# Mixer A's lowest score level by multiplied rows and a product with ones; small products traced one at a time between large ones; an even spread of steps

## The chip, the cores and the metric

The kernel runs on one core of a Trainium2 chip. A core has TensorE (matrix products), VectorE, ScalarE and GpSimd (element-wise work), and SyncE, which issues DMAs. The metric is the device time of one execution in microseconds (us); the median of several runs is compared. In the profile PE is TensorE's products, PEld its weight loads, DVE is VectorE, ACT ScalarE, POOL GpSimd, and SP SyncE. A line such as L588 is line 588 of the kernel before.

## What is computed

The reference is a trunk of two layers over 512 tokens of width 2048, in float32. Layer A is a gated linear recurrence (HGRN2), layer B attention with a forget gate. Each layer is: RMS norm, one input projection, the mixer with 16 heads of 128, a norm per head, times SiLU of a gate, an output projection, plus the residual.

```python
# layer A, per head; blocks of HG_BLOCK = 16 tokens, state S carried from block to block
b = jnp.cumsum(gc, axis=-2)                                  # gc: log of the forget gate
diff = b[..., :, None, :] - b[..., None, :, :]
decay = jnp.exp(jnp.where(mask, diff, -jnp.inf))             # mask: s <= t
A = jnp.einsum('bhtd,bhsd,bhtsd->bhts', qc, kc, decay)
o = A @ vc + (qc * jnp.exp(b)) @ S
# layer B, per head
s = q @ k.T * d**-0.5 + F[t] - F[s]                          # s <= t
o = softmax(s) @ v
```

So a score of layer A is the sum over the 128 channels d of q[t,d] k[s,d] exp(b[t,d] - b[s,d]).

## The kernel before

**Large groups.** Everything lies transposed: channels on the 128 partitions, the 512 tokens along the free dimension. A projection is cut into groups of 512 output columns (`group`, L220 to L249). A group runs over 16 steps of the contraction, here called k-steps (`kt`). Weights and activations are each split into a rounded high half and the low rest (`split`, L439: a cast on ScalarE, a subtraction on VectorE), and a product is three: high-high, high-low, low-high. A k-step has 4 output banks `gm0` to `gm3` times 3 products = 12 products of 512 columns. After the last k-step each bank is evacuated by VectorE or ScalarE (`evac`).

**The output products** (`out_product`, L833) have one such group, in which finished heads are split and prepared (`y_split`, `quick_prep`), and six pairs of groups by Strassen's scheme (`quick`, L269), with 256-column products whose weights are seven sums of quarters. VectorE makes these sums (`w_sums`, L153, tile `wm`) and they are split into `w7h` and `w7l`.

**Order.** For A the groups are `q0 v0 q1 q2 v1 q3 g0 q4 v2 q5 q6 v3 q7 g1 g2 g3`, for B `v0 q0 q1 q2 v1 g0 q3 q4 v2 g1 q5 q6 v3 q7 g2 g3`; a q group brings q and the key or gate side of two heads, a v group the values of four, a g group the gates of four. An output product ends each phase.

**Mixers as steps.** A head's mixer is a Python generator (`mix_a`, L606; `mix_b`, L922), and each `yield` ends a step. After each k-step `group` adds `rate` to `due` and calls `pump`, which runs that many steps of the first two open heads in turn, the second from when the first has reached "half". RATE_A is 2 and RATE_B 1. What a step traces stands in the program there. The order of tracing is a priority: a scheduler then places each engine's instructions by it and by when it reckons that their inputs are ready, so the products of a step can come later than they are traced, and some stand alone between large ones. `need` runs steps early where an evacuation wants a buffer, `flush` (L103) runs what is left at the end of a phase.

**Scores of A.** Tokens of a window of 128 are compared at levels: 1 (neighbours in groups of 4), 4, 16, 64, and then across windows. For d = 0 to 3 tokens back, level 1 forms q times the decay (tile `pr`, L628; tile `e` holds the decays of one, two and three tokens), splits q, `pr` and k, and multiplies them on TensorE: per window 3 products of 320 columns (L588 to L590), a full 128 by 320 table, of which `put_scores` (L575) copies the entries d tokens back into `at` with predicated copies under masks. Then q and k are multiplied by their decays in place (L640, L645) for the next level. Levels 4 and 16 have 3 products of 192 columns for each window, level 64 three of 128 columns for each of two windows; the scores across windows go to `ah` and `al`. `attend` (L425) multiplies by the values with 12 products, and `out_norm` (L396) sums squares with a product by `ones` (`sum_parts`, L328) and writes `Y[h]` (L407).

**Banks.** Four PSUM banks (`mx`, L71) serve all of the mixers' products; the four `gm` banks serve the large groups.

## Time and profile before

| | |
|---|---|
| median of 3 runs | 2014.63 us (2012.73 to 2015.29) |
| the profiled execution | 2013.94 us, its span 2012.2 us |
| instructions | 28874 |
| chain that ended last, by engine | PE 84%, DVE 7%, DMA 4%, issue 2%, ACT 1%, POOL 1% |
| large products (L238 to L244) in that chain | 17% + 17% + 17% + 6% + 6% + 6% |
| predicated copies (L583) | 448, 108.8 us of VectorE |
| granted TensorE clock | 0.994 of full speed |

The span is the time from the first to the last instruction of the program; the execution's time also has what lies around it. A busy share is the part of the span in which an engine had an instruction under way. A row of the timeline gives start, length, engine, line, operation, result and operands, and shapes; a bracket at its end gives the idle time before it and what ended it. A row of waits gives who waited for whom, the sum, the number of times and the longest. TensorE's products overlap, so the length of one is more than the time that it takes from its neighbours; the distance between two starts shows that.

### The profile page before, as it was taken

Reading aid. Unit: us, or ns where it says so; the run is one execution under the profiler, and the core shown is the slowest. Engines: PE = TensorE matmul, PEld = TensorE weight load, DVE = VectorE, ACT = ScalarE, POOL = GpSimd, SP = SyncE. Lnnn points to the kernel's source line nnn. Section 1 sums busy time; section 2 is a strip of 40 time slices with the busy share of each in tenths; the row PEclk is TensorE's granted clock in tenths of the full one; section 3 lists DMA queues with packets and bytes.
Section 4 is the critical chain, followed back from the end, with each engine's and each line's share of the span. In section 5 each row is a group of like instructions: output and inputs, shape, how many; then the busy total and the mean of one; then the engine's idle time right before and its main releaser. Section 6 shows DMA issues by size and latency. Waiting matters only on the chain.

```text
span 2012.2 us, 28874 instructions
## 1 busy us (share of the span) xinstructions
PE 1978.6 (98%) x10218; PEld 1696.5 (84%) x10218; DVE 1558.8 (77%) x3321; ACT 1130.1 (56%) x2311; POOL 172.8 (9%) x301
## 2 busy tenths in 40 slices
PE   9999999999999999989999999999999999999898
PEld 7888888888888888869987888888888888888898
DVE  7968987979798889698873677776766676688877
ACT  5646655657566466654443555655555556576332
POOL 3303110202122030000000000000000000000000
PEclk9999999999999999999999999999999999999999
DMA  5222222222222222244433222333233232223443
GB/s 189 74 87 82 74 84 75 83 79 79 84 74 74 74 84 84 84 142 140 149 118 95 94 87 87 95 89 95 84 89 93 92 95 89 90 84 111 132 156 105
DMA packets 61696, 195.01 MB, mean 97 GB/s; under 512 B 7904, under 2 KB 8032, under 8 KB 61552
## 3 DMA queue, kind: packets, MB, share of 16 engines
q1 hardware_dynamic: 61408, 193.17, 30.8%
q8 instruction: 80, 1.31, 0.3%
q14 instruction: 64, 0.52, 0.1%
q10 hardware_dynamic: 144, 0.01, 0.0%
HBM read 184.73 MB, written 8.42 MB: 96 GB/s over the span
## 4 chain that ended last, share of the span: by engine, by line
PE 84%; DVE 7%; DMA 4%; issue 2%; ACT 1%; POOL 1%; SPq 0%; DVEq 0%; ACTq 0%; POOLq 0%
PE gm L244 17%; PE gm L242 17%; PE gm L243 17%; PE gm L238 6%; PE gm L240 6%; PE gm L239 6%; DMA wr<-in_wb_q 2%; DVE w7l L441 2%; PE mx L590 2%; PE mx L589 2%; PE mx L588 1%; DMA wr<-in_wa_q 1%; PE mx L435 1%; PE mx L436 1%; PE mx L434 1%
## 5 line engine op out<-in xcount | busy, mean ns | idle before, releaser
L242 PE MATMUL gm<-xh,wh 128*128 128x512 f32 x1664 | 650.6, 392 | 0.1
L243 PE MATMUL gm<-xl,wh 128*128 128x512 f32 x1664 | 649.8, 391 | 0.0
L244 PE MATMUL gm<-xh,wl 128*128 128x512 f32 x1664 | 610.3, 392 | 1.1 <-DVE wl L441 1.1
L242 PEld LDWEIGHTS gm<-xh,wh 128*128 128x128 f32 x1664 | 313.1, 188 | 63.1 <-ACT wh L440 0.3
L243 PEld LDWEIGHTS gm<-xl,wh 128*128 128x128 f32 x1664 | 313.2, 188 | 62.7
L244 PEld LDWEIGHTS gm<-xh,wl 128*128 128x128 f32 x1664 | 311.3, 188 | 63.6 <-DVE wl L441 2.3
L440 ACT CAST wh<-wr 128x512 fp32r<-128x512 f32 x288 | 177.3, 620 | 155.7 <-PE gm L243 113.8
L441 DVE TENSOR_TENSOR wl<-wr,wh 128x512 fp32r<-128x512 f32 x288 | 204.7, 714 | 66.8 <-ACT wh L440 56.8
L147 ACT ACTIVATE wh<-wr,v_b_norm_w 128x256 fp32r<-128x256 f32 (+1 forms) x192 | 111.7, 584 | 186.4 <-PE gm L243 152.3
L148 DVE SCALAR_TENSOR_TENSOR wl<-wr,v_b_norm_w,wh 128x256 fp32r<-128x256 f32 (+1 forms) x192 | 109.3, 571 | 133.5 <-ACT wh L147 128.3
L239 PE MATMUL gm<-wl,xh 128*128 128x512 f32 x512 | 200.7, 392 | 0.0
L240 PE MATMUL gm<-wh,xl 128*128 128x512 f32 x512 | 200.2, 392 | 0.0
L238 PE MATMUL gm<-wh,xh 128*128 128x512 f32 x512 | 180.5, 392 | 1.5 <-DVE q L552 1.5
L147 ACT ACTIVATE wh<-wr,v_kv_norm_w 128x256 fp32r<-128x256 f32 (+1 forms) x192 | 110.1, 574 | 65.2 <-PE gm L240 48.3
L148 DVE SCALAR_TENSOR_TENSOR wl<-wr,v_kv_norm_w,wh 128x256 fp32r<-128x256 f32 (+1 forms) x192 | 109.3, 571 | 42.1 <-ACT wh L147 41.5
L583 DVE COPY_PREDICATED at<-masks,mx 128x128 f32<-128x128 uint8 (+4 forms) x448 | 108.8, 297 | 13.4 <-PE mx L590 13.0
L942 POOL TENSOR_SCALAR_AFFINE_SELECT s<-s 128x128 f32<-128x128 f32 x64 | 28.5, 445 | 1029.1 <-DVE s L941 1028.6
L238 PEld LDWEIGHTS gm<-wh,xh 128*128 128x128 f32 x512 | 95.9, 188 | 20.4 <-DVE q L552 1.8
L240 PEld LDWEIGHTS gm<-wh,xl 128*128 128x128 f32 x512 | 96.2, 188 | 19.0
L239 PEld LDWEIGHTS gm<-wl,xh 128*128 128x128 f32 x512 | 96.3, 188 | 18.8
L440 ACT CAST w7h<-wr 128x768 fp32r<-128x768 f32 x48 | 40.1, 835 | 100.7 <-PE mx L296 38.2
L440 ACT CAST kh<-k 128x512 fp32r<-128x512 f32 (+1 forms) x96 | 56.3, 587 | 44.1 <-PE mx L589 19.7
(225 smaller groups left out, 3852.6 us busy)
## 6 DMA issues: line engine op xcount, KB each, us to landing
wr<-in_wb_qk SPq DMA_DIRECT2D x64, 512.0 KB, 3.5
wr<-in_wa_qf SPq DMA_DIRECT2D x62, 512.0 KB, 3.5
wr<-in_wa_v SPq DMA_DIRECT2D x32, 512.0 KB, 3.5
wr<-in_wa_g SPq DMA_DIRECT2D x32, 512.0 KB, 3.5
wr<-in_wb_v SPq DMA_DIRECT2D x32, 512.0 KB, 3.5
wr<-in_wb_g SPq DMA_DIRECT2D x32, 512.0 KB, 3.5
wr<-in_wa_q SPq DMA_DIRECT2D x24, 512.0 KB, 3.5
wr<-in_wb_q SPq DMA_DIRECT2D x24, 512.0 KB, 3.6
```

The costliest lines, as they stand in the source:

```text
L147: S.activation(h[:, c], r[:, c], AF.Copy, scale=w[:, kt : kt + 1])
L148: V.scalar_tensor_tensor(l[:, c], r[:, c], w[:, kt : kt + 1], rd(h)[:, c], op0=ALU.mult, op1=ALU.subtract)
L238: PE.matmul(banks[j], xh, h, start=f, stop=False)
L239: PE.matmul(banks[j], xh, l, start=False, stop=False)
L240: PE.matmul(banks[j], xl, h, start=False, stop=e)
L242: PE.matmul(banks[j], h[:, c], Xh[kt], start=f, stop=False)
L243: PE.matmul(banks[j], h[:, c], Xl[kt], start=False, stop=False)
L244: PE.matmul(banks[j], l[:, c], Xh[kt], start=False, stop=e)
L440: S.copy(h, src)
L441: return V.tensor_sub(l, src, rd(h))
L583: V.copy_predicated(out, mv, data)
L589: PE.matmul(lv[:, base : base + n], kh[:, c], ml, start=False, stop=False)
```

## The change

**Level 1 of mixer A** no longer uses the 128 by 320 tables. VectorE forms the products q[t,c] k[t-d,c] times the decay for every token (`p0` for d = 0, `pr` for d = 1, 2, 3: 512 and 768 columns). `half_parts` adds the upper 64 partitions to the lower ones and puts the high halves of the sums on 64 partitions and the low rests on the other 64. Three products with `ones` (512, 512 and 256 columns) then sum over the partitions, which leaves each dot product on all 128 partitions, and `put_scores` copies all four windows at once.

**Small products.** `later` puts a mixer's product in a list instead of tracing it. After each large product `one_small` traces the first of the list, if at least LAG_A = 6 or LAG_B = 12 large products have passed since it was put there. Before a head's next step `settle` traces those of its products that are left. Steps are cut so that the reader of a product stands in a later step than the product: `mix_b` is split in `scores`, `probs`, `turn_over` and `turned`, and `attend` and `out_norm` are two steps.

**Steps** are pumped after each bank's three products (`rate / 4`) instead of after each k-step, and the rates are 1.7 and 0.95 instead of 2 and 1.

```diff
-RATE_A, RATE_B = 2, 1
+RATE_A, RATE_B = 1.7, 0.95
+
+LAG_A, LAG_B = 6, 12
...
+    small, now, large = [], [None], [0]
+
+    def later(fn, *args, **kw):
+        small.append((now[0], fn, args, kw, large[0] + cur["lag"]))
+
+    def one_small():
+        large[0] += 1
+        if small and small[0][4] <= large[0]:
+            _, fn, args, kw, _ = small.pop(0)
+            fn(*args, **kw)
+
+    def settle(task):
+
+        own = [s for s in small if s[0] == task]
+        small[:] = [s for s in small if s[0] != task]
+        for _, fn, args, kw, _ in own:
+            fn(*args, **kw)
...
             try:
+                now[0] = tasks[turn[0]][0]
+                settle(now[0])
                 next(tasks[turn[0]][1])
...
-                    PE.matmul(banks[j], h[:, c], Xh[kt], start=f, stop=False)
-                    PE.matmul(banks[j], h[:, c], Xl[kt], start=False, stop=False)
-                    PE.matmul(banks[j], l[:, c], Xh[kt], start=False, stop=e)
+                    three = ((h[:, c], Xh[kt]), (h[:, c], Xl[kt]), (l[:, c], Xh[kt]))
+                for i, (a, b) in enumerate(three):
+                    PE.matmul(banks[j], a, b, start=f and i == 0, stop=e and i == 2)
+                    one_small()
                 if e:
                     evac(j, banks[j])
-            due[0] += rate
-            pump(int(due[0]))
-            due[0] %= 1
+                due[0] += rate / 4
+                pump(int(due[0]))
+                due[0] %= 1
...
+    def half_parts(x, hl):
+
+        half = P // 2
+        V.tensor_add(x[:half], x[:half], x[half:])
+        S.copy(hl[:half], x[:half])
+        V.tensor_sub(hl[half:], x[:half], rd(hl)[:half])
...
-            PE.matmul(o[:, t], vh[:, w, :], ah[:, a], start=w == 0, stop=False)
...
+            later(PE.matmul, o[:, t], vh[:, w, :], ah[:, a], start=w == 0, stop=False)
...
-        kh, kl = k_split(h, k)
-        pr = mt("pr", (P, NW, 192), 1)
...
-                win_scores(lv, 0, w0 + i, kh, kl, mh[:, c], ml[:, c], 320)
-                for d, c0 in ((0, 0), (1, P), (2, P + 96), (3, P + 160)):
-                    put_scores(at, lv, w0 + i, 1, c0, T, 1, d, d)
-                yield
+
+        p0 = rd(mt("kl", (P, T), 2, F32R))
+        pr = mt("pr", (P, 768), 1)
+        V.tensor_mul(p0, q, k)
+        for d, c0 in ((1, 0), (3, 384), (2, 512)):
+            n = 4 - d
+            o = view(pr, c0, [[n, P], [1, n]])
+            V.tensor_mul(o, view(q, d, [[4, P], [1, n]]), view(e, (d - 1) * T + d, [[4, P], [1, n]]))
+            V.tensor_mul(o, o, view(k, 0, [[4, P], [1, n]]))
+        yield
+        hl, hl0 = m_tiles(h)
+        half_parts(p0, hl0[:, :T])
+        half_parts(pr, hl)
+        V.tensor_mul(view(q, 0, [[4, P], [1, 4]]), view(q, 0, [[4, P], [1, 4]]), view(e, 0, [[4, P], [T + 1, 4]]))
+        kv = view(k, 0, [[4, P], [1, 3]])
+        V.tensor_mul(kv, kv, view(e, 2 * T + 3, [[4, P], [-T, 3]]))
+        yield
+        for x, w, parts in (
+            (hl0, T, ((0, 0),)),
+            (hl, T, ((1, 0), (3, 384))),
+            (hl[:, T:], 256, ((2, 0),)),
+        ):
+            lv = lv_bank()
+            later(PE.matmul, lv[:, :w], ones, x[:, :w], start=True, stop=True)
             yield
+            for d, c0 in parts:
+                put_scores(at, lv, 0, NW, c0, (4 - d) * 32, 1, d, d)
...
                     win_scores(lv, (w - w0) * 192, w, kh, kl, mh[:, c], ml[:, c], 192)
+                yield
                 for d, c0 in ((1, 0), (2, 96), (3, 160)):
                     put_scores(at, lv, w0, 2, c0, 192, m, d, d)
-                yield
...
         o = attend(h, ah, al)
+        yield
         out_norm(h, o, vec["a_out_norm_w"])
...
-        last = None
-        for w in range(NW):
-            s = probs(w)
+        bk = scores(0)
+        yield
+        s0 = probs(0, bk)
+        bk = scores(1)
+        yield
+        last = probs(1, bk)
+        pt = turn_over(0, s0)
+        reached.add(("half", h))
+        yield
+        for w in (2, 3):
+            turned(w - 2, pt)
+            bk = scores(w)
             yield
...
+            s, last = last, probs(w, bk)
+            pt = turn_over(w - 1, s)
+            yield
+        turned(2, pt)
+        pt = turn_over(3, last)
+        yield
+        turned(3, pt)
```

## The prediction

> **What bounds the kernel now.** I read first the busy shares on the page, then who TensorE waited for, then its timeline, which shows what one product costs from start to start.

> ```profile
> span 2012.2 us, 28874 instructions
> ## 1 busy us (share of the span) xinstructions
> PE 1978.6 (98%) x10218; PEld 1696.5 (84%) x10218; DVE 1558.8 (77%) x3321; ACT 1130.1 (56%) x2311; POOL 172.8 (9%) x301
> ```

> ```profile
> PE mx L295 <- ACT w7h L440: 15.5, 2, 8.4
> ...
> PE gm L238 <- DVE q L552: 1.5, 2, 1.0
> ```

> ```profile
> 602.13 0.39 PE L239 MATMUL gm<-wl,xh 128*128 128x512 f32 x1
> 602.36 0.30 PE L588 MATMUL mx<-mh,kh 128*128 128x320 f32 x1
> 602.50 0.31 PE L589 MATMUL mx<-ml,kh 128*128 128x320 f32 x1
> 602.65 0.31 PE L590 MATMUL mx<-mh,kl 128*128 128x320 f32 x1
> 602.80 0.39 PE L240 MATMUL gm<-wh,xl 128*128 128x512 f32 x1
> 603.03 0.40 PE L238 MATMUL gm<-wh,xh 128*128 128x512 f32 x1
> ...
> 606.22 0.25 PE L588 MATMUL mx<-mh,kh 128*128 128x192 f32 x1
> ...
> 606.87 0.41 PE L240 MATMUL gm<-wh,xl 128*128 128x512 f32 x1
> 607.12 0.39 PE L238 MATMUL gm<-wh,xh 128*128 128x512 f32 x1
> ...
> 609.87 0.25 PE L588 MATMUL mx<-mh,kh 128*128 128x192 f32 x1
> 609.95 0.42 PE L238 MATMUL gm<-wh,xh 128*128 128x512 f32 x1
> 610.21 0.39 PE L239 MATMUL gm<-wl,xh 128*128 128x512 f32 x1
> ...
> 849.86 0.39 PE L242 MATMUL gm<-xh,wh 128*128 128x512 f32 x1
> ...
> 894.23 0.28 PE L296 MATMUL mx<-xl,w7h 128*128 128x256 f32 x1
> 894.35 0.28 PE L297 MATMUL mx<-xh,w7l 128*128 128x256 f32 x1
> 902.99 0.58 PE L295 MATMUL mx<-th,w7h 128*128 128x256 f32 x1 [8.36 <-ACT w7h L440]
> ```

> The second column is a modelled length, so I use the distance of starts. A 512-column product takes 0.23 us, a 320-column one 0.147 (0.44 for three), a 256-column one 0.12. TensorE has a product running practically always, and of its waits the large ones are two (15.5 us) in the output products, where VectorE prepares quarter sums; the mixers' own stretches have little (1.5 us for q). So inside the mixers time is bought only by giving TensorE less to do, and where it waits (894.35 to 902.99) the VectorE decides.

> ```profile
> 700.00:725.00 25.00, 25.00 (x121) 21.13 (x120) 16.62 (x42) 15.85 (x34) 0.00 (x0) 1.00 0.28 85
> 725.00:750.00 25.00, 24.83 (x121) 20.75 (x120) 24.58 (x53) 18.33 (x41) 16.44 (x22) 1.00 0.26 66
> 800.00:825.00 25.00, 25.00 (x125) 21.20 (x124) 18.09 (x42) 14.73 (x33) 0.00 (x0) 1.00 0.25 75
> 825.00:850.00 25.00, 25.00 (x112) 20.71 (x111) 18.89 (x31) 15.73 (x30) 0.00 (x0) 1.00 0.31 97
> ```

> Columns are length, TensorE, weight loads, VectorE, ScalarE, GpSimd, granted clock. The last row holds almost only 512-column products: 25.0 / 111 = 0.225 us each. TensorE is full in all four rows, while VectorE is full in one and idle for a quarter to a third in others: second in line, and full in bursts.

> **Level 1 on TensorE.** Removed per head are 12 products of 320 columns: 12 x 0.147 = 1.76 us. Added are three with `ones`, of 512, 512 and 256 columns: 2 x 0.225 + 0.12 = 0.57. Saved: 1.19 us a head, 16 heads **19.0 us**. TensorE orders all other work there, so nothing hides this; it is the term that I trust.

> **Level 1 on VectorE and ScalarE.** The number after the bar is busy time, the next the mean length in ns.

> ```profile
> L441 DVE TENSOR_TENSOR w7l<-wr,w7h 128x768 fp32r<-128x768 f32 x48 | 45.7, 952 | 1.6 <-ACT w7h L440 1.5
> L333 DVE TENSOR_TENSOR t<-t 64x512 f32<-64x512 f32 x64 | 44.1, 690 | 24.8 <-ACT t L400 22.0
> L335 DVE TENSOR_TENSOR sl<-t,sl 64x512 fp32r<-64x512 f32 x64 | 43.5, 685 | 1.9
> ...
> L583 DVE COPY_PREDICATED at<-masks,mx 128x128 f32<-128x128 uint8 x128 | 36.3, 297 | 11.3 <-PE mx L590 11.2
> ...
> L583 DVE COPY_PREDICATED at<-masks,mx 128x192 f32<-128x192 uint8 x64 | 22.8, 371 | 1.8 <-PE mx L590 1.8
> ```

> The three products with e, over their shapes:

> ```profile
> L628 DVE TENSOR_TENSOR pr<-q,e 128x384 f32<-128x384 f32 (+2 forms) x48 | 25.6, 569 | 0.3 <-ACT e L617 0.3
> ```

> A low half of 512 columns is 0.69 us, one of 768 is 0.95; by their slope 384 columns are 0.55 and 256 are 0.42. Before, a head has the low half of k (0.69), three products with e (3 x 0.569 = 1.71), four low halves (2 x (0.55 + 0.42) = 1.94) and 16 predicated copies. After, it has q times k (0.69), those three products and three more in place by k, taken at the same price (3.41 in all), two additions and two subtractions over 64 partitions (2 x 0.69 + 2 x 0.95 = 3.28; L333 and L335 show the price at 64 partitions) and four predicated copies of 512 to 128 columns. From 0.297 at 128 and 0.371 at 192 columns, 1.16 ns a column, these are 0.74 + 0.59 + 0.45 + 0.30 = 2.08. The 16 narrow ones are 4.75 us at 0.297 each, if each is paid whole: then the sum goes from 9.1 to 9.5, +0.4 us a head. But instructions in a row overlap, narrow ones most; if a narrow copy costs only its columns (1280 in all at 1.16 ns, 1.5 us) the sum grows by 3.6. Between these ends I take +1.5, nearer the first because each instruction has a fixed part: 24 us over the 16 heads. ScalarE loses casts of 512, twice 384 and twice 256 columns and gets one of 512 and one of 768: less work there.

> [...]

> What hides VectorE's growth is TensorE's time for a head, 849.86 / 16 = 53 us (849.86 is the first start of the output product). The cover is thin where VectorE is full (24.58 of 25) and wide where it is not (16.62).

> **Products traced singly.** 88 products a head and mixer pair (54 in A, 34 in B), 1408 in all, may stand alone between large ones. A run of six 192-column ones stretched the row of starts by 607.12 - 606.22 - 0.225 = 0.675, 0.113 each; a single one by 610.21 - 609.87 - 0.225 = 0.115. No gain for TensorE, therefore: the small one is done early, but the large one behind it is held up (0.26 instead of 0.23). Rows end at 0.01 us, so up to 5 ns each may hide: 0 to 7 us lost, and I take **2**. A product that stands behind more large ones finds its inputs ready more often, which can remove waits like the 1.5 us for q; banks held longer (four `mx`) can make as many: -3 to +3, taken as **-1.5**.

> **Steps.** Counting the yields of the code, a head of A has 21 steps instead of 20, one of B 12 instead of 11, and the rates fall by 15% and 5%. The last step of A's head 15 moves from k-step 3 to k-step 10 of group g2, with g3 still behind it; that of B from k-step 5 to 11 of g3, the last group. Neither phase gets steps in `flush`. GpSimd's sums in A and the one DMA of a head in B (`fb`, on SP's queue behind weights that are loaded two chunks ahead) move with their steps; GpSimd is idle for most of the span (9% busy), so nothing queues there. A step now falls between the evacuations of one group too, with up to 5 us of VectorE work ahead of the next bank's release (the step with the half sums); TensorE goes on with the banks that are free, and the row of 1.5 us for `gm L238` prices that wait today.

> **Where the saving can be lost.** The output product after A waits 8.36 us for `w7h`, which hangs on VectorE.

> ```profile
> 830.83 0.75 DVE L407 SCALAR_TENSOR_TENSOR y<-t,v_a_out_norm_w,t 128x512 f32<-128x512 f32 x1
> ```

> That is the last head of A done, 19 us ahead of the output product. TensorE's saving brings the later heads' q and k sooner as well, so of itself it costs none of this lead. VectorE's 24 us do: where it is full they find no room, elsewhere they do. If half finds none, the heads end 12 us later against the output product, and the 13 idle us of 800 to 850 (the last two rows), in which VectorE can split finished heads ahead, take up most of that. I take **+3** for the longer wait; -2 if all finds room, +11 (24 - 13) if nothing does, +15 with steps traced too late. After B the same wait is 15.5 - 8.4 = 7.1 us. VectorE has no more to do there, but the last steps are traced 6 x 12 x 0.225 = 16 us later: **0**, from -4 to +8 (half of the 16).

> **Sum.** -19.0 + 2 - 1.5 + 3 = -15.5 us. The profiled execution took 2013.94 us (span 2012.2 and 1.7 around it), so 1998.4; the median of the three runs is 0.7 higher: 2014.6 - 15.5 = **1999**. About 0.2% (4 us) is what a measurement can tell from no change.

> **Rivals.**
> - *Given back in the output product.* Nothing of VectorE's 24 us finds room before 800, A's heads end beside the output product's start, and the wait for `w7h` grows from 8.4 to some 20 us: -19 + 2 + 11 = -6, 2009. For it: the row 24.58 of 25; against it: a quarter idle in three of four rows.
> - *The even steps help VectorE.* Its bursts flatten into the idle quarters, the 1.5 us and most of the 8.4 go: -19 - 1.5 - 6.5 = -27, 1988. For it: full and two-thirds-full rows stand side by side. Against it: part of the idle time comes from a head's chain through the engines, which a rate does not shorten.
> - *TensorE isn't the bound.* Its busy time is modelled and weight loads fill only 84%; if the rest were slack, fewer products would change nothing: 2014. Against it: large starts keep their 0.225 us through whole rows, with a product of any kind between them paid in full.
> - *Slower: VectorE becomes the pace of mixer A.* Level 1 costs it 3.6 us more a head (the upper end), 58 us over the phase, and three quarters (43) find no room. Less the 13 idle us, 30 come out as waits in the output product, against 17 saved: 2028. It decides from 30 us of late work on. For it: VectorE is full in bursts already; against it: the upper end takes a narrow copy to have no fixed part.

> [...]

> **Chances.** Forecast (1993 to 2004) 0.66; given back 0.14; more than the products 0.10; TensorE not the bound 0.04; VectorE's pace 0.06. Two thirds of "given back" lie more than 0.2% below: faster 0.66 + 0.10 + 0.09 = 0.85, same 0.05 + 0.04 = 0.09, slower 0.06. The range goes from 1987 (all terms at their low ends: -19 - 3 - 2 - 4 = -28) to 2011, most of "given back"; it leaves out the slower case and the unchanged one.

> **What would show it.** The level-1 products go from 192 of 320 columns to 48 with `ones`; large starts stay 0.225 apart; VectorE's busy time rises by 6 to 58 us, 24 expected; the last L407 of A lies 0 to 15 us ahead of the output product's start, and the wait for `w7h` there is 8 to 15 us. I am wrong if small products alone cost clearly more than 0.115, if TensorE waits over 10 us in A's groups, or if a wait for `w7h` passes 20.

## The result and the profile after

The changed kernel is **slower**: 2044.55 us in the median of four runs (2040.69 to 2048.64) against 2013.68 for the kernel before, measured beside it (2010.52 to 2015.29). The ratio is 1.0153, 95% interval 1.0141 to 1.0165. The forecast was 1999, its range 1987 to 2011. The profiled execution took 2040.69 us.

The page of the changed kernel, its span and its busy shares:

```profile
span 2039.0 us, 28382 instructions
...
PE 1974.2 (97%) x10074; PEld 1675.7 (82%) x10074; DVE 1604.3 (79%) x3177; ACT 1114.4 (55%) x2263; POOL 173.3 (9%) x301
```

TensorE has 144 products fewer, as it should, and VectorE is busy 45.5 us longer (1604.3 - 1558.8). To see where the time lies I cut the span at the first starts of groups and compare the length of each stretch with what its products take when nothing hinders them. The prices are distances of starts in full rows: 0.227 us for 512 columns, 0.175 for 384, 0.146 for 320, 0.120 for 256, 0.112 for 192, 0.111 for 128. What is left over I call **excess**: waits, half clock, rounding.

| stretch | before: length, products, excess | after: length, products, excess |
|---|---|---|
| q0 of A | 53.3, 46.0, 7.3 | 52.8, 46.0, 6.8 |
| A from v0 to its output product | 796.6, 789.0, **7.6** | 819.8, 770.1, **49.7** |
| output product of A | 180.9, 164.5, 16.3 | 180.0, 164.5, 15.5 |
| B from v0 to its output product | 796.2, 794.5, 1.7 | 796.9, 792.6, 4.3 |
| output product of B | 185.3, 164.8, 20.5 | 189.4, 166.7, 22.7 |

The products of A shrank by 18.9 us, and the stretch still grew by 23.2: 42 us of excess are new there. B and its output product add 4.8. Who waits in A? The rows of waits of the changed kernel, TensorE's alone, for 53 to 853 us (who waited for whom, us in total, times, longest):

```profile
PE mx L103 <- DVE al L470: 11.2, 5, 3.5
PE mx L103 <- DVE at L612: 4.9, 5, 1.2
PE gm L265 <- ACT v L450: 3.9, 3, 1.8
PE gm L265 <- DVE wl L470: 3.5, 5, 1.3
PE mx L103 <- DVE mh L365: 2.5, 1, 2.5
```

L103 is now the line of a product that comes from the list, and L470 `split`. The same query on the kernel before gives 1.5 us for q and one row more:

```profile
PE mx L588 <- ACT mh L440: 1.0, 3, 0.6
```

No tile stands out: `attend` waits for `al`, the next score for a bank that the copies into `at` still read, the large group for its bank or its weights. Most of these rows name VectorE, each at another place (`v` is a bank that ScalarE evacuates). The longest case, in the timeline of the changed kernel, and behind it the end of A:

```profile
383.60 0.28 DVE L470 TENSOR_TENSOR al<-at,ah 128x128 fp32r<-128x128 f32 x1
383.80 0.68 DVE L470 TENSOR_TENSOR wl<-wr,wh 128x512 fp32r<-128x512 f32 x1
383.88 0.40 PE L103 MATMUL mx<-ah,vh 128*128 128x512 f32 x1
384.51 0.69 DVE L365 TENSOR_TENSOR ml<-kl,ml 64x512 fp32r<-64x512 f32 x1
385.23 0.95 DVE L363 TENSOR_TENSOR pr<-pr 64x768 f32<-64x768 f32 x1
386.22 0.86 DVE L668 TENSOR_TENSOR k<-k,e 128x384 f32<-128x384 f32 x1
387.12 0.89 DVE L470 TENSOR_TENSOR al<-mx,ah 128x384 fp32r<-128x384 f32 x2
387.73 0.50 PE L103 MATMUL mx<-al,vh 128*128 128x512 f32 x1 [3.46 <-DVE al L470]
...
388.52 1.88 DVE L415 TENSOR_TENSOR z<-gm,rstd 128x512 f32<-128x512 f32 x3
...
390.00 0.63 PE L265 MATMUL gm<-xh,wl 128*128 128x512 f32 x1
390.43 0.63 PE L265 MATMUL gm<-xh,wh 128*128 128x512 f32 x1
390.86 0.63 PE L265 MATMUL gm<-xl,wh 128*128 128x512 f32 x1
...
840.12 0.74 DVE L436 SCALAR_TENSOR_TENSOR y<-t,v_a_out_norm_w,t 128x512 f32<-128x512 f32 x1
...
872.63 0.39 PE L265 MATMUL gm<-xh,wh 128*128 128x512 f32 x1
...
926.07 0.58 PE L317 MATMUL mx<-th,w7h 128*128 128x256 f32 x1 [8.67 <-ACT w7h L469]
```

Read VectorE's rows from 384.51: three instructions of the *next* head's level 1 (halves of 512 columns, halves of 768, k times its decay) stand in its queue ahead of the `al` that the first head's products need. They take 2.6 us of the 3.46 that TensorE waits. Then the products from 390.00 on start 0.43 us apart instead of 0.23. The windows of the same kernel show why (columns as in the prediction; the seventh is the granted clock):

```profile
384.00:388.00 4.00, 0.54 (x3) 0.27 (x2) 3.87 (x7) 1.78 (x4) 0.00 (x0) 1.00 0.00 0
388.00:390.00 2.00, 1.73 (x7) 1.18 (x7) 2.00 (x5) 1.43 (x4) 0.00 (x0) 0.90 0.23 18
390.00:392.00 2.00, 2.00 (x6) 1.61 (x5) 1.94 (x3) 2.00 (x5) 0.00 (x0) 0.50 0.64 244
392.00:394.00 2.00, 2.00 (x8) 1.64 (x8) 2.00 (x6) 2.00 (x5) 0.00 (x0) 0.75 0.00 0
```

The wait of 3.46 us costs another 1.7 us at half clock (0.50 from 389.60 to 393.01). From 53 to 853 us the starts show about 36 us of excess at products that waited and about 12 in slow starts of products that did not (before: under 4 each). Only a part of the 12 is half clock: A has three stretches of 3.41 us of it (from 218.93, 389.60 and 775.30 us), at most 5.1 us lost.

The last rows of the timeline show where the loss is *not*. A's last head is done at 840.9, 32 us ahead of the output product (18 by the same ends before; the prediction's 19 goes from the start of the row), and the wait for `w7h` is 8.67 us (8.36 before).

### The profile page after: what moved, and what is told of

Same layout as the page of the kernel before. It is cut to its first block, busy times and chain, and to the rows that moved or that the text cites. A ratio compares the mean times of both kernels' runs of the same rounds, so it can differ in the third digit from the quotient of the medians.

```text
span 2039.0 us, 28382 instructions
## 1 busy us (share of the span) xinstructions
PE 1974.2 (97%) x10074; PEld 1675.7 (82%) x10074; DVE 1604.3 (79%) x3177; ACT 1114.4 (55%) x2263; POOL 173.3 (9%) x301
## 4 chain that ended last, share of the span: by engine, by line
PE 76%; DVE 17%; issue 3%; DMA 3%; ACT 1%; DVEq 0%; SPq 0%; ACTq 0%
PE gm L265 61%; PE mx L103 5%; DVE wl L470 2%; DMA wr<-in_wb_q 2%; PE mx L110 2%; DVE at L612 2%; DVE w7l L470 1%; PE mx L317 1%; PE gm L319 1%; PE mx L318 1%; PE mx L319 1%; PE gm L318 1%; PE gm L317 1%; DVE kl L470 1%; DVE ml L470 1%
## 5 line engine op out<-in xcount | busy, mean ns | idle before, releaser
L470 DVE TENSOR_TENSOR wl<-wr,wh 128x512 fp32r<-128x512 f32 x288 | 204.7, 714 | 72.7 <-ACT wh L469 57.9
L612 DVE COPY_PREDICATED at<-masks,mx 128x128 f32<-128x128 uint8 (+5 forms) x256 | 97.3, 403 | 11.2 <-PE mx L103 6.1
L469 ACT CAST w7h<-wr 128x768 fp32r<-128x768 f32 x48 | 40.1, 835 | 102.4 <-PE mx L318 48.9
L469 ACT CAST ah<-mx 128x384 fp32r<-128x384 f32 (+2 forms) x128 | 46.4, 373 | 45.9 <-PE mx L103 20.9
```

The costliest lines, as they stand in the source:

```text
L469: S.copy(h, src)
L470: return V.tensor_sub(l, src, rd(h))
L612: V.copy_predicated(out, mv, data)
```

## The experiments

All times are medians, all ratios against runs of the kernel before on the same chip. "Pace" is what the text below comes to: k-steps of TensorE per head, the steps of a head divided by the rate. A has 240 k-steps behind its first group, 15 a head; the pace cannot be slower than that for long.

| run | level 1 | steps / rate = pace | VectorE busy in A | products | excess in A | time |
|---|---|---|---|---|---|---|
| before | old | 20 / 2 = 10.0 | 683 | 789.0 | 7.6 | 2013.7 |
| e16_before_slow | old | 20 / 1.4 = 14.3 | 678 | 789.0 | 4.1 | 2013.7 |
| e7_fill | old, 4 products more | 20 / 2 = 10.0 | 717 | 789.0 | 18.5 | 2023.4 |
| e2_old_level1 | old | 23 / 1.7 = 13.5 | 675 | 789.0 | 8.7 | 2024.1 |
| e1_level1 | new | 18 / 2 = 9.0 | 728 | 770.1 | 67.3 | 2053.0 |
| e18_level1_130 | new | 18 / 1.3 = 13.8 | 725 | 770.1 | 36.7 | 2019.9 |
| e14_level1_slow | new | 18 / 1.25 = 14.4 | 725 | 770.1 | 23.7 | 2010.9 |
| after | new | 21 / 1.7 = 12.4 | 726 | 770.1 | 49.7 | 2044.6 |
| e3_pump_kstep | new | 12.4 | 727 | 770.1 | 56.7 | 2050.2 |
| e4_no_later | new | 12.4 | 727 | 770.1 | 53.3 | 2043.7 |
| e9_lag | new | 12.4 | 726 | 770.1 | 49.4 | 2045.9 |
| e13_fine_steps | new | 26 / 2.1 = 12.4 | 727 | 770.1 | 57.3 | 2050.6 |
| e8_slow_steps | new | 21 / 1.45 = 14.5 | 724 | 770.1 | 28.9 | 2020.6 |
| e10_rate | new | 14.5 | 725 | 770.1 | 29.3 | 2021.4 |
| e5_full_split | new, 128 partitions | 12.4 | 700 | 779.3 | 30.0 | 2032.7 |
| e6_full_split_old_steps | new, 128 partitions | 9.0 | 697 | 779.3 | 40.1 | 2036.6 |
| e17_full_split_slow | new, 128 partitions | 14.4 | 696 | 779.3 | 33.2 | 2026.5 |
| e15_full_split_slow_g | the same, one product on GpSimd | 14.4 | 694 | 779.1 | 30.4 | 2027.2 |
| e11_a_slow_b_old | new, 128 partitions | 14.5 | 690 | 779.3 | 17.7 | 2018.6 |
| e12_slower | new, 128 partitions | 21 / 1.35 = 15.6 | 682 | 777.4 | 26.9 | 2034.5 |

### Which part of the change

**Level 1 alone** in the kernel before: `half_parts` and the new level 1 of the diff above, its products traced at once.

```diff
-                win_scores(lv, 0, w0 + i, kh, kl, mh[:, c], ml[:, c], 320)
...
+            PE.matmul(lv[:, :w], ones, x[:, :w], start=True, stop=True)
```

> Level 1 as dot products alone, in the kernel before (its rates, its pumping after the k-step, no list of small products). Theory L (level 1 puts 45 us more on VectorE, and that alone makes TensorE wait in mixer A): 2030 to 2045, A's excess over its products 35 to 50 us, VectorE 44 us busier than before. Theory P (the new places of steps and products do it): the 19 us of products are saved, 1993 to 2000, A's excess under 15 us.

**The changed kernel with the old level 1**, its products through `later`, a `yield` ahead of their copies.

```diff
-            later(PE.matmul, lv[:, :w], ones, x[:, :w], start=True, stop=True)
...
+                win_scores(lv, 0, w0 + i, kh, kl, mh[:, c], ml[:, c], 320)
+                yield
```

> The changed kernel with level 1 as before (tables of 320 columns), so the list of small products, the pumping after each bank and the rates alone. Theory L: near before, 2008 to 2020, A's excess under 15 us. Theory P: the changed kernel's waits stay and the 19 us of products come back, 2045 to 2065, A's excess 35 to 50 us.

**Steps after each k-step**, and **products traced at once**, in the changed kernel:

```diff
-                due[0] += rate / 4
-                pump(int(due[0]))
-                due[0] %= 1
+            due[0] += rate
+            pump(int(due[0]))
+            due[0] %= 1
```

> The changed kernel with steps pumped once after a k-step again, so that no step stands between the evacuations of one group; rates and list kept. Theory E (a part of P: banks are released late because steps are traced between evacuations): the excess at group ends falls from 29 to under 12 us, 2015 to 2027. If the place of the pump doesn't matter: 2036 to 2050, the excess at group ends above 20 us.

```diff
     def later(fn, *args, **kw):
-        small.append((now[0], fn, args, kw, large[0] + cur["lag"]))
+        fn(*args, **kw)
```

> The changed kernel with every small product traced at once where its step stands, instead of through the list; rates and pumping kept. Theory S (a part of P: single products at fixed places make TensorE stand in line behind inputs that come late): A's excess falls below 20 us, 2000 to 2015. Theory L: within 8 us of the changed kernel, 2033 to 2050.

Measured: 2052.98 (1.0197, interval 1.0176 to 1.0218), 2024.12 (1.0060, 1.0043 to 1.0077), 2050.19 (1.0187, 1.0167 to 1.0208) and 2043.73 (1.0155, 1.0135 to 1.0175). Level 1 alone loses all and more, beyond theory L's range (67.3 us of excess where 35 to 50 were expected). TensorE's waits of the first of these kernels, 53 to 853 us, show the same kinds of lateness; the evacuation of a large bank (`z`) leads:

```profile
PE gm L242 <- DVE z L393: 8.7, 3, 3.5
PE mx L595 <- DVE at L590: 6.8, 5, 2.1
PE mx L442 <- DVE al L448: 6.2, 5, 2.5
PE mx L595 <- ACT mh L447: 5.9, 5, 1.8
```

With the old level 1, A is as good as before (8.7 of excess), and what this kernel loses lies elsewhere: of the 8.4 us of its span, 1.3 in the output product of A and 6.1 in B and its output product, where TensorE's wait for `w7h` is 12.2 us instead of 7.2. In the kernel that traces its products at once it is 7.7. With the list, B and its output product are 6 to 7 us longer than without it (986.3 and 987.6 us against 980.6), and the last head is done 18 us behind the start of the output product instead of 13 (10 before). But the list is not the only way to that wait. Two kernels further down trace B's products at once, at a rate of 1 per k-step, and wait 11.7 and 11.6 us; the row of the first:

```profile
PE mx L324 <- ACT w7h L476: 11.7, 1, 11.7
```

What sets this wait in B is open. The single products themselves cost little (B's own excess is 4.3 us with the list and 3.9 without, 1.7 before). In A the changed kernel without the quarters has 56.7 us of excess and without the list 53.3: neither is the cause there.

### Amount of work, or its kind

**Level 1 split on all partitions**, in the changed kernel and in the first of these runs: no additions of halves, but six products with `ones` instead of three.

```diff
-        hl, hl0 = m_tiles(h)
-        half_parts(p0, hl0[:, :T])
-        half_parts(pr, hl)
+        hl, ll = m_tiles(h)
+        split(p0, hl0, ll0)
+        split(pr, hl, ll)
...
-            later(PE.matmul, lv[:, :w], ones, x[:, :w], start=True, stop=True)
+            later(PE.matmul, lv[:, :w], ones, x[:, :w], start=True, stop=False)
+            later(PE.matmul, lv[:, :w], ones, y[:, :w], start=False, stop=True)
```

> The changed kernel, but level 1 splits the 512 and 768 products on all 128 partitions: no additions of halves, the split kept as a high and a low half, and six products with `ones` instead of three. VectorE loses two additions a head (0.69 + 0.95 us, some 1.6 us of the 2.7 that level 1 had grown by), TensorE gains 0.57 us a head (9 us in all). Theory V, amount of VectorE work in mixer A decides: the excess over the products in A (49.7 us in the changed kernel) falls by well more than the 9 us of new products, to 10 to 30 us, and the time is 2020 to 2035. Theory O, the kind of the new instructions or their order decides and not their amount: the excess stays at 45 to 55 us, the 9 us are paid on top, 2048 to 2055.

> The same level 1 on 128 partitions in the kernel before, with the steps and products placed as there (the first experiment's level 1 gave 67 us of excess in A and 2053). Theory V: excess in A falls to 15 to 40 us, 2010 to 2035; near the lower end this is as fast as the kernel before. Theory O: excess stays over 60 us, 2058 to 2065.

**Useless products in the kernel before**; they change nothing in the output.

```diff
+        for _ in range(4):
+            V.tensor_mul(view(pr, 0, [[1, T]]), q, k)
```

> The kernel before with four products of 128x512 more per head of A on VectorE, of no use (they are written where the real products go later), 4 x 0.6 us x 16 heads, some 40 us of VectorE, as much as the new level 1 added; TensorE's products unchanged. Theory V, the amount of VectorE work decides: A's excess goes from 7.6 to 35 to 65 us and the time to 2040 to 2075. Theory O: these are independent instructions of a known price and stand in one place, the excess stays below 20 us and the time below 2025.

Measured: 2032.72 (1.0103, 1.0088 to 1.0118), 2036.58 (1.0121, 1.0106 to 1.0136) and 2023.38 (1.0056, 1.0039 to 1.0073). The row of the added products, of the last of these kernels, has the count that was meant, at 0.68 us each instead of 0.6:

```profile
L627 DVE TENSOR_TENSOR pr<-q,k 128x512 f32<-128x512 f32 x64 | 43.7, 682 | 1.0 <-ACT k L565 0.7
```

VectorE's busy time in A rises by 34 us there, and the excess by 11. Less work helps too: 26 us less take 20 us off the excess of the changed kernel, of which 9 go to the added products. But 14 us more than before, in the form of level 1, cost 32 (e6, at 9 k-steps a head instead of 10), and 34 us more, as independent products, cost 11. The first two runs came out near theory V's bounds (30.0 and 40.1 us of excess, for 10 to 30 and 15 to 40), the third inside theory O's. Amount counts, and it is not all; both theories were too simple.

### Where the products stand, and the pace

**Slower steps and a longer distance**, then each of the two by itself:

```diff
-RATE_A, RATE_B = 1.7, 0.95
+RATE_A, RATE_B = 1.45, 0.95
...
-LAG_A, LAG_B = 6, 12
+LAG_A, LAG_B = 14, 12
```

> The changed kernel with A's steps at 1.45 per k-step instead of 1.7 and its small products held back 14 large products instead of 6. Theory T, TensorE waits since small products are placed before VectorE has made their inputs: A's excess falls from 49.7 to below 30 us, unless the last heads then end too late for the output product; 2025 to 2035. Theory V, VectorE's throughput in its full bursts decides wherever the products stand: excess 45 to 60, 2040 to 2055.

> The changed kernel with one number changed: A's small products are held back 14 large products instead of 6 (steps at 1.7 per k-step as in the changed kernel). Both numbers together took A's excess from 49.7 to 28.9 and the time to 2021. Theory Lag, the products stood too early behind the VectorE step that makes their inputs and a longer distance is what helped: excess below 35, 2020 to 2030. Theory Rate, VectorE's work was packed into too short a stretch: excess stays at 43 or more, 2038 to 2046.

> The changed kernel with the other number changed: A's steps at 1.45 per k-step, the products held back 6 large ones. Theory Rate: excess below 35, 2020 to 2030. Theory Lag: excess 43 or more, 2035 to 2046, somewhat below the changed kernel at most.

Measured: 2020.63 (1.0039, 1.0023 to 1.0055) together, 2045.91 (1.0159, 1.0144 to 1.0174) for the distance, 2021.42 (1.0032, 1.0020 to 1.0045) for the rate. This is the clearest pair of the study: the rate takes back 23 us, the distance nothing. Theory T was right in its excess (28.9, below 30), not in its time (2025 to 2035), and wrong in its reason.

**The same work in finer steps at the same pace**: five `yield`s more in level 1.

```diff
-RATE_A, RATE_B = 1.7, 0.95
+RATE_A, RATE_B = 2.1, 0.95
...
         V.tensor_mul(p0, q, k)
+        yield
...
             V.tensor_mul(o, o, view(k, 0, [[4, P], [1, n]]))
-        yield
+            yield
...
         half_parts(p0, hl0[:, :T])
+        yield
         half_parts(pr, hl)
+        yield
```

> The changed kernel with level 1's VectorE work of a head spread over seven steps instead of two (products with e and k one shape at a time, halves one tensor at a time), 26 steps a head instead of 21, and A's rate raised to 2.1, so that a head still takes 12.4 k-steps. Amount of work and pace are those of the changed kernel. Theory Lump, the two long steps of level 1 (5 us of VectorE each) stand ahead of evacuations and of the other head's splits: excess in A below 35, 2022 to 2032. Theory Pace, heads are traced faster than VectorE works: excess stays at 43 to 55, 2038 to 2050.

2050.60 (1.0188, 1.0170 to 1.0205), with 57.3 us of excess: not the lumps.

**The pace in the other two kernels**: 1.25 and 1.3 with level 1 alone, 1.4 in the kernel before.

```diff
-RATE_A, RATE_B = 2, 1
+RATE_A, RATE_B = 1.25, 1
```

> The kernel before with the new level 1 alone (18 steps a head, at rate 2 it gave 67 us of excess in A and 2053) and A's steps at 1.25 per k-step: 14.4 k-steps a head, as in the run with 1.45, instead of 9. Theory Pace: excess falls to 25 to 35 and the time to 2010 to 2020, B and its output as before. Theory List, the slower pace helps only together with steps at quarters and single products: excess above 45, 2028 or more.

> The new level 1 alone at 1.3 steps per k-step instead of 1.25. Counting the yields, at 1.25 four steps of A are forced at the evacuation of q6 because a later head must be through, at 1.3 none, and the list of steps runs dry before the end of group q1 and almost nowhere else. Theory Pace, best where steps neither run dry nor are forced: A's excess 18 to 26, 2004 to 2013, at or below the run at 1.25. If excess rises with any step of the rate (1.25 to 2 gave 24 to 67, 0.58 us per 0.01), it is 26 to 27 and the time 2011 to 2016.

> The kernel before with one number changed: A's rate 1.4 instead of 2 (20 steps, 14.3 k-steps a head instead of 10). Theory Pace: VectorE's old work fits at either pace, A's excess stays 4 to 12, 2008 to 2018. If slow steps by themselves are worth 20 us, whatever level 1 is, it goes well below the kernel before, which has only 7.6 us to lose there; if they push work past the output product's start, its w7h wait grows and it is slower, 2020 or more.

Measured: 2010.87 (0.9985, 0.9976 to 0.9995), 2019.88 (1.0032, 1.0020 to 1.0045) and 2013.67 (0.9998, 0.9987 to 1.0009). One number, 2 to 1.25, makes 42 us for the new level 1; 2 to 1.4 makes nothing for the time of the old one. The run at 1.3 missed both of its forecasts: A's excess is 36.7 us, where 18 to 27 were expected. So the excess does not follow the pace smoothly: 13 us lie between 13.8 and 14.4 k-steps a head. Two windows of A, first of the changed kernel, then of level 1 alone at 1.25, then of the kernel before at 1.4:

```profile
353.00:453.00 100.00, 95.16 (x452) 78.82 (x452) 87.29 (x187) 55.24 (x115) 9.87 (x16) 0.98 0.25 79
553.00:653.00 100.00, 95.53 (x458) 78.79 (x458) 97.00 (x196) 63.86 (x135) 27.84 (x41) 1.00 0.24 74
```

```profile
353.00:453.00 100.00, 99.97 (x485) 83.59 (x484) 97.35 (x202) 62.47 (x132) 14.88 (x26) 1.00 0.24 79
553.00:653.00 100.00, 97.03 (x469) 80.44 (x468) 95.08 (x197) 63.96 (x145) 25.48 (x38) 1.00 0.24 74
```

```profile
353.00:453.00 100.00, 100.00 (x494) 84.94 (x493) 89.70 (x218) 63.65 (x137) 15.50 (x27) 1.00 0.26 80
553.00:653.00 100.00, 100.00 (x499) 85.20 (x498) 86.06 (x221) 63.22 (x148) 20.02 (x35) 1.00 0.26 80
```

VectorE 97% full goes with TensorE at 95.5% in one row and at 99.97% in another. A full VectorE alone is therefore no sign of loss here; in the rows from 384.51 the loss came because what TensorE needed next stood behind 2.6 us of another head's work. In the changed kernel's first row VectorE has 13% idle, and TensorE loses as much as in the second: the work comes in bunches. That fits the count of the yields: at 1.7 the list of open heads runs dry in q1, q4 and q5 (17 to 19 of 27 or 28 steps there are used), at 1.45 hardly. That bunches do the harm is argued from this, not shown by a run. What is left at the best pace, from the waits of level 1 alone at 1.25, 53 to 853 us:

```profile
PE gm L238 <- DVE q L559: 3.7, 1, 3.7
PE gm L244 <- DVE wl L448: 2.4, 4, 1.0
PE gm L239 <- DVE wl L448: 2.2, 4, 0.9
```

The kernel before at 1.4 has no row at all there. At the same pace the new level 1 saves 18.9 us of products and has 19.6 us more of excess: the gain is real, and new waits, most of them for VectorE by the rows above, take it all back.

### Both together

**A at 1.45 with the full split, B traced as before**; **slower still**; and the full split in the kernel before at 1.25, with q times k **on GpSimd** or not:

```diff
-RATE_A, RATE_B = 1.7, 0.95
+RATE_A, RATE_B = 1.45, 1
-LAG_A, LAG_B = 6, 12
+LAG_A, LAG_B = 14, 0
...
     def later(fn, *args, **kw):
+        if cur["lag"] == 0:
+            return fn(*args, **kw)
```

> A with both numbers (1.45 and 14) and level 1 split on 128 partitions; in B steps and products at once and after each k-step at rate 1, as before the change. Terms: A by the pair 28.9 us of excess, by the full split some 10 less at 9.2 more of products if the two gains add, so A about 795 to 800; B's two phases together 928 to 930 as in the run that traced B's products at once, instead of 934. Theory: 2010 to 2017, no difference that matters to the kernel before. If the two gains in A rest on the same waits, excess stays near 29 and the time is 2020 to 2026.

```diff
-RATE_A, RATE_B = 1.45, 1
+RATE_A, RATE_B = 1.35, 1
-LAG_A, LAG_B = 14, 0
+LAG_A, LAG_B = 20, 0
```

> The one beside it with A's steps slower still, 1.35 per k-step, and products held back up to 20 large ones. If the rate is what frees VectorE, A's excess falls by another 5 to 10 us and the time is 2003 to 2012, faster than the kernel before; if the last heads now end after the output product's start, its wait for w7h passes 15 us and the time is 2015 to 2030.

```diff
-RATE_A, RATE_B = 2, 1
+RATE_A, RATE_B = 1.25, 1
...
-        V.tensor_mul(p0, q, k)
+        G.tensor_mul(p0, q, k)
```

> As the run beside it, with level 1 split on 128 partitions and q times k multiplied on GpSimd instead of VectorE: per head VectorE loses 1.6 + 0.6 us, TensorE gains 0.57, GpSimd gains one product of 128x512 (1.3 us by its additions of that shape). Theory Pace and amount together: A's excess 8 to 18 at 779 of products, 2003 to 2013, as fast as the kernel before or faster. If GpSimd's product holds up VectorE or comes late in the head's chain, excess above 25, 2018 or more.

> The full split of level 1 on 128 partitions, all on VectorE, in the kernel before with A's steps at 1.25 per k-step: the previous run without GpSimd's product. If GpSimd's product of q and k (1.7 us, and GpSimd's additions of the next head behind it grew from 1.3 to 2.2 us) was what cost time there, A's excess falls from 30 to 8 to 18 and the time to 2005 to 2013. If the full split does not fit this pace, excess stays above 22 and the time at 2016 or more.

Measured: 2018.57 (1.0022, 1.0012 to 1.0031), 2034.50 (1.0104, 1.0089 to 1.0119), 2027.22 (1.0069, 1.0054 to 1.0084) and 2026.49 (1.0060, 1.0047 to 1.0072). In the first the gains in A add (17.7 us of excess), but the products grew by 9.2 and B kept its long wait for `w7h`: the time is above the 2010 to 2017 that were expected. In the second the pace is slower than the 15 k-steps that there are: by the count of the yields 14 steps are forced at the evacuation of q6, and its excess between 550 and 600 us is some 10; neither of its two forecasts came true, though its wait for `w7h` behind A did grow to 13.1 us. The last two are misses: the full split gains little from the pace without the list and the quarters, 40 to 33, and GpSimd's product is not why. The waits of the last kernel, 53 to 853 us, are new ones, for the sum of squares behind a bank:

```profile
PE mx L336 <- DVE sl L335: 9.1, 2, 4.5
PE gm L242 <- DVE q L559: 3.5, 2, 1.8
```

Two waits of 4.5 us are 9 of its 33 us of excess. Where such single collisions fall, at which end of which group, decides over some 10 us from kernel to kernel; the pace does not explain that.

## Why the prediction was wrong

- **Products of level 1: right.** -19.0 us forecast, -18.9 measured, 48 products with `ones`, large starts 0.227 apart where nothing waits.
- **VectorE's growth: mis-sized.** Taken +1.5 us a head, 24 in all; measured 43 in A, 2.7 a head, inside the bounds of 0.4 to 3.6. The rows of the changed kernel, by shape:

```profile
L365 DVE TENSOR_TENSOR mh<-pr,mh 64x768 fp32r<-64x768 f32 x16 | 20.4, 1278 | 0.5
...
L363 DVE TENSOR_TENSOR pr<-pr 64x768 f32<-64x768 f32 x16 | 15.3, 954 | 0.5
...
L612 DVE COPY_PREDICATED at<-masks,mx 128x384 f32<-128x384 uint8 x16 | 11.8, 740 | 0.8
L612 DVE COPY_PREDICATED at<-masks,mx 128x512 f32<-128x512 uint8 x16 | 11.8, 740 | 6.3 <-PE mx L103 6.1
L612 DVE COPY_PREDICATED at<-masks,mx 128x256 f32<-128x256 uint8 x16 | 11.7, 732 | 0.3
```

  The new instructions cost what was put down, or a little more (the last subtraction 1.28 instead of 0.95, the copies 2.6 instead of 2.1). The term failed on what goes away. I chose between 4.75 us a head for the 16 narrow copies (each paid whole) and 1.5, nearer the first. The timeline of the kernel before would have told, by its starts:

```profile
602.75 0.29 DVE L583 COPY_PREDICATED at<-masks,mx 128x64 f32<-128x64 uint8 x1
602.88 1.03 DVE L407 SCALAR_TENSOR_TENSOR y<-t,v_a_out_norm_w,t 128x512 f32<-128x512 f32 x1
603.83 0.29 DVE L583 COPY_PREDICATED at<-masks,mx 128x64 f32<-128x64 uint8 x1
603.96 0.55 DVE L692 TENSOR_TENSOR q<-q,t 128x384 f32<-128x384 f32 x1
```

  A copy of 64 columns is 0.29 long and takes 0.13 from what follows. Over all of them the median distances are 0.198, 0.165, 0.131 and 0.098 for 128, 96, 64 and 32 columns: 2.4 us a head, where the +1.5 implies about 3.6. With 2.4 the sum gives +2.7, as measured.
- **The step that failed: "Where the saving can be lost".** VectorE's growth was priced at the output product alone (+3, at most +15), and inside A at nothing: late work would find idle time or show at the end, and "TensorE goes on with the banks that are free". It did not go on: in the wait of 2.52 us for `mh` that ends at 107.16 TensorE started no product, and the large ones behind it in its order came from 108.45 on, with no wait of their own. The runs put 42 us there, and 0.3 us into the wait for `w7h` of A. The sign that I had named for being wrong, over 10 us of waits in A's groups, came. The 1.5 us of the row for `gm L238` priced a queue on VectorE that was shorter by 2.7 us a head.
- **The slower rival had the engine and missed the place.** It asked for 43 us of late work and let 30 come out as waits in the output product, 2028. The heads are in fact done earlier against it (32 us ahead).
- **Even steps: no gain in A over the kernel before.** At quarters or at k-steps, the changed kernel loses (49.7 and 56.7 us of excess). The *rate* mattered, which I had counted only for when the last steps are traced. With 18 or 21 steps for 20, the diff changes a head's pace from 10 to 12.4 k-steps; of the paces that were tried, the new level 1 lost least at 14.4.
- **Waits of the mixers, -1.5 forecast (-3 to +3):** lost in the 42.
- **Singles: right.** +2 forecast (0 to 7); with the list B has 0.5 us more excess than without, A 1.1 more than before with the old level 1.
- **B: 0 forecast (-4 to +8), 4.8 measured,** inside the bounds. The way named for them fits: the last head is done 18 us behind the start of the output product instead of 10, and the wait for `w7h` is 12.2 us instead of 7.2. That this comes from the later steps alone is not shown.
- **"TensorE isn't the bound": no.** Slower by 42 us of its waits, it is.

Shown: the loss comes with the new level 1 in A, as waits of TensorE that are mostly for VectorE, and hangs on the pace of its steps. **Open:** why the new level 1 is so much more sensitive to the pace than the old one, which at 10 k-steps a head has only 7.6 us of excess, and 4.1 at 14.3. The amount of work explains a part (11 us for 34 of it). The length of the steps, the list, the quarters and the distance of the products do not; the additions of halves alone do not (30 to 40 us of excess without them). That the scheduler reckons the new chain shorter than it runs, and so writes TensorE's order too early, would fit, but was not tried. Level 1 alone ran at 9 k-steps a head against 10 before, so its 67 us hold some pace too; but at 12.4, slower than before, there are still 49.7.

Is a version better than both? Level 1 alone at 1.25 is 0.15% faster than the kernel before (0.9976 to 0.9995), less than the 0.2% set as what can be told from no change, and 1.3 in its place is 0.3% slower. I would not keep it.

## What to carry to other kernels

Work taken off a full engine is worth only what the second engine leaves of it: here 19 us of products against 43 us of VectorE, at 86% of the stretch already. A busy share below 100% was no cover: from 353 to 453 us VectorE is busy for 87.29 us of 100, and TensorE's wait of 3.46 us for `al` lies there. Price late work where the next consumer stands, not at the end of the phase. And when an edit changes the number of steps a head has, its rate has to be set anew, for the pace was worth more (23 to 42 us) than the edit.

## What the hardware showed that I had not expected

- **What a wait cost beyond its length hung on where it fell.** After 3.46 us without a product the granted clock was 0.50 for 3.41 us, and 512-column products started 0.43 us apart. TensorE was not idle throughout ahead of every half clock: here half clock follows 3.41 us in which it was busy for 1.72 and had one wait of 1.60:

```profile
1038.13:1041.54 3.41, 1.72 (x12) 1.33 (x11) 3.41 (x6) 0.90 (x2) 0.00 (x0) 1.00 0.70 252
1041.54:1044.96 3.42, 3.42 (x17) 3.42 (x17) 3.42 (x7) 2.37 (x4) 0.00 (x0) 0.50 0.00 0
```

```profile
L621 POOL TENSOR_TENSOR e<-g 128x511 f32<-128x511 f32 x16 | 34.6, 2162 | 241.4 <-DVE k L647 122.9 <-DVE g L578 118.5
...
L635 POOL TENSOR_TENSOR t<-q,k 128x512 f32<-128x512 f32 x16 | 27.8, 1739 | 76.8 <-DVE g L578 53.4 <-DVE z L397 23.4
```

  In the kernel that differs by this product alone the addition took 1422:

```profile
L621 POOL TENSOR_TENSOR e<-g 128x511 f32<-128x511 f32 x16 | 22.8, 1422 | 290.9 <-DVE k L647 175.0 <-DVE g L578 113.3 <-ACT mh L447 2.6
```
